# One more pair of query tiles computed ahead, and a list scheduler that counts an engine's own result delay

## The chip, the cores and the metric

The kernel runs on one core of one Trainium2 chip. Time is device time of one execution in microseconds, and a kernel is given by the median of its runs; the kernel before took 1141.6 us (three runs, 1141.54 to 1143.01). TensorE (PE) does the matrix products and loads its weights on a queue of its own (PEld); VectorE (DVE), ScalarE (ACT) and GpSimd (POOL) do the elementwise work; SyncE (SP) issues most DMAs and POOL issues the accumulating ones. Each engine works through its own instructions in the order in which the program lists them, and waits on semaphores where an operand is not there yet.

## The reference

Two layers over 1024 tokens of width 1024, all in float32:

```
x = layer_norm(a*x + gla_mixer(x))          # gated linear attention, 4 heads, chunks of 64
k, v = shared_kv(x)                         # 3 groups x 2 heads of 128, rope on k
x = layer_norm(a*x + dilated_mixer(x, k, v))

def dilated_mixer(x, k, v):
    q, gate = split(x @ w_in)               # q: 3 groups x 8 heads x 128; gate: 1024
    q = rope(q) * 128**-0.5
    for g, (window, dilation) in enumerate(((128, 1), (512, 4), (2048, 16))):
        o[g], lse[g] = windowed softmax attention of q[:, g] over k[:, g], v[:, g]
    o = sum(softmax(lse over g)[g] * o[g])
    return (o * silu(gate)) @ w_out
```

The change lies in the second layer: in how `q` is projected, and in the order of the work everywhere.

## The kernel before

**Arithmetic.** A float32 product is made of three fast ones: each operand is split in a rounded upper part and the rest (`wh`, `wl` for weights, `x1h`, `x1l` for the activations), and `wh*xh + wh*xl + wl*xh` is summed in PSUM. The rest of a weight is made in one of two ways: by a subtraction on DVE or POOL (`split_lo`), or, with `added=True`, by a negated copy on ACT onto which a DMA from POOL then adds the weight from memory (line 664).

**Stages.** The gated linear attention takes the first 355 us, its layer norm and the start of the second layer run to about 440, the projections of V and sums of activation columns (`sums()`: tiles `T1` to `T4`, and `s`) to about 515. From there to 702 stand the *pairs*: two weight tiles are multiplied with all activations together by a scheme of seven products instead of eight (`load_pair` makes the weight sums, `seven` does the products, whose PSUM tiles are called `sev`). A pair takes 7 x 12 = 84 matmuls of 128x512, where two tiles one by one (`project`, PSUM tiles `acc`) take 96. Three pairs are the keys; the others are the query tiles that `EARLY` names as (head, head, group). The roped result (`rope`, into the page `pair`) goes to DRAM (`kd`, `qd`). From 702 to 1040 runs the attention, one head after another: `q_proj(u)` reads the query tiles that lie in `qd` and projects the missing ones itself; `scores(u)` makes the products with the keys (`lv`), the maxima and sums (`sts`), and sends them through DRAM (`std`) to another layout (`nat`), where the weights of the three groups (`ew`, `cw`) are made, which go back through `cwd`; `attend(u)` scales and transposes the probabilities (`ms<-ident,P`) and multiplies with V (`po`); `g_proj` projects the gate. The output projection and the last layer norm end the program.

**Order.** The program is not written in the order in which it runs. Every operation is recorded by `Sched`, with a cost per engine, its dependences, and a rank; `order` (line 263) then fills the engines like a list scheduler: of the operations that are ready it takes the one with the earliest start, then the lowest rank. An operation on another engine's result starts `pad` later than that result's end; one on a result of its own engine starts at once. `vp` operations may go to DVE or POOL, `va` and `vap` ones to ACT too, and the scheduler picks the engine. `issue` then emits all of them through one line, so the profile shows L462 for everything, and tiles are told apart by name.

Of the kernel before, what the change touches and what calls it, by code (L numbers as in the profile page):

```python
# [34 lines left out]
       ("POOL", "ACT"): 0.07, ("POOL", "DVE"): 0.07, ("POOL", "PE"): 0.08, ("SP", "POOL"): 0.15}  # L35
WEIGHTS, EVAC, WARM = 3000, 1000, 4
AHEAD = 0.35
RUNS, GATHER = 0.3, 1.0
QUEUED, ISSUE, ADDED = 2.4, 0.9, 1.7
EARLY = [(0, 1, 2), (2, 3, 2), (1, 3, 1), (4, 5, 2), (6, 7, 2), (4, 5, 1), (6, 7, 1)]  # L40


class Buf:
# [93 lines left out]


class Op:
    __slots__ = ("engs", "calls", "reads", "writes", "prio", "deps", "nuse", "cost", "t0", "t1", "eng", "func",  # L140
                 "first", "succ", "left", "seq", "port", "least")


class Sched:
# [81 lines left out]
    def depend(self):  # L226
        hist = {}
        self.bufs = []
        for i, o in enumerate(self.ops):
            deps = set()  # L230
            for views, wr in ((o.reads, False), (o.writes, True)):
                for v in views:
                    w, r = hist.setdefault(id(v.buf), ([], []))
                    lo, hi = v.span()
                    for j, l2, h2 in (w + r if wr else w):
                        if j != i and lo < h2 and l2 < hi:
                            deps.add(j)
            for v in o.writes:
                lo, hi = v.span()
                for h in hist[id(v.buf)]:  # L240
                    h[:] = [x for x in h if not (lo <= x[1] and x[2] <= hi)]
            for v in o.writes:
                hist[id(v.buf)][0].append((i,) + v.span())
            for v in o.reads:
                hist[id(v.buf)][1].append((i,) + v.span())
            o.deps = deps
            o.first = []
            for v in o.reads + o.writes:
                b = v.buf
                if b.users is None:  # L250
                    b.users = []
                    self.bufs.append(b)
                if not b.users or b.users[-1] is not o:
                    b.users.append(o)
                    o.first.append(b)
        for o in self.ops:
            o.succ, o.left = [], len(o.deps)
        for i, o in enumerate(self.ops):
            for d in o.deps:
                self.ops[d].succ.append(o)  # L260


    def order(self):
# [6 lines left out]
        for b in self.bufs:  # L270
            if True:
                t = tags.setdefault((id(b.pool), b.tag), {"bufs": b.bufs, "queue": [], "next": 0, "live": []})
# [53 lines left out]
        while n_done < len(ops):  # L326
            best = None
            for e in self.ENG:
                cand = None
                for o in ready[e]:  # L330
                    if o.t0 is not None:
                        continue
                    r = soft = o.least
                    for d in o.deps:
                        q = ops[d]
                        t = q.t1 + (0.0 if q.eng == e else self.pad.get((q.eng, e), self.lat))
                        r = max(r, t)
                        soft = max(soft, t + (AHEAD if e == "PE" and q.eng in ("ACT", "DVE", "POOL") else 0.0))
                    if o.first:
                        t = alloc_time(o)  # L340
                        r = max(r, t)
                        soft = max(soft, t + (AHEAD if e == "PE" and t > 0 else 0.0))
                    if r >= INF:
                        continue
                    k = o.engs.index(e)
                    st = max(free[e], r, port) if o.port[k] else max(free[e], r)
                    if any(max(free[q], r) <= st and c < o.cost[o.engs.index(e)] for q, c in zip(o.engs, o.cost)):
                        continue

                    key = (max(st, soft), o.prio)  # L350
                    if cand is None or key < cand[0]:
                        cand = (key, o, st)
                if cand is not None:
                    (late, pr), o, st = cand
                    if best is None or (late, pr) < best[0]:
                        best = ((late, pr), o, e, st)
            if best is None:
                left = [o for o in ops if o.t0 is None]
                raise RuntimeError(f"no instruction can be issued; {len(left)} left, first {left[0].calls[0][0]} "
                                   f"{[v.buf.name for v in left[0].writes]}")  # L360
            _, o, e, st = best
            c = o.cost[o.engs.index(e)]
            if o.func is not None and e == "ACT":
                new = act_set(o.func, cur_set)
                if new != cur_set:

                    c += 1.3 if cur_set else 0.0
                    cur_set = new
            o.t0, o.eng = st, e
            if o.calls[0][0] == "dma_start":  # L370
                added = e == "POOL"
                dma_free = max(dma_free, st + ISSUE * added) + c * (ADDED if added else 1.0)
                o.t1 = dma_free + (QUEUED if added else 1.7)
                free[e] = st + (ISSUE if added else 0.37)
            else:
                o.t1 = st + c
                free[e] = o.t1
                if o.port[o.engs.index(e)]:
                    port = o.t1
            for b in o.first:  # L380
                if b.placed:
                    continue
                b.placed = True
                tg = tags[id(b.pool), b.tag]
                tg["next"] += 1
                if len(tg["live"]) >= tg["bufs"]:
                    old = min((x for x in tg["live"] if all(u.t0 is not None for u in x.users)),
                              key=lambda x: max(u.t1 for u in x.users))
                    tg["live"].remove(old)
                tg["live"].append(b)  # L390
            for p in {id(v.buf.pool) for v in o.reads + o.writes}:
                pool_users[p]["left"] -= 1
                pool_users[p]["end"] = max(pool_users[p]["end"], o.t1)
            for q in o.engs:
                ready[q].remove(o)
            for s in o.succ:
                s.left -= 1
                if s.left == 0:
                    for q in s.engs:
                        ready[q].append(s)  # L400
            done.append(o)
            n_done += 1
# [216 lines left out]
def trunk(tc, xT, wP, wA, wA12, wAv3, w2, wO, wK, wV0, wV12, wB, wOB, par_d,  # L619
# [10 lines left out]
    t1 = S.pool("t1", side="right")  # L630
# [15 lines left out]
    def hs(half):  # L646
        return slice(half * 512, half * 512 + 512)
# [36 lines left out]
    def project(piece, xs, evac, halves=(0, 1), added=False):  # L684
        w = load_w(piece, added)
        for half in halves:
            acc = ps.tile([128, 512], F32, name="acc", bufs=2)
            proj_cols(w, xs, hs(half), acc)
            with S.later(-EVAC):
                evac(half, acc)  # L690
# [495 lines left out]
    vd0 = [dram.tile([128, T], F32, name=f"vd0{c}") for c in range(2)]  # L1186
    qd = {(u, g): dram.tile([128, T], F32, name=f"qd{u}{g}") for *us, g in EARLY for u in us}

# [20 lines left out]
    def layer_b(xs, early):  # L1209
# [17 lines left out]
        def rope(pg, g, half, acc):  # L1227
            r = hs(half)
            t1 = small("t1", "t1", 2)
            S.vector.tensor_mul(t1, acc, cosT[:, r])  # L1230
            t2 = small("t2", "t2", 2)
            S.scalar.copy(t2[0:64, :], acc[64:128, :])
            S.scalar.copy(t2[64:128, :], acc[0:64, :])
            S.vp.tensor_mul(t2, t2, sinT[:, r])
            S.vp.tensor_add(to_group(pg, g, half), tok_view(t1, g), tok_view(t2, g))
# [166 lines left out]
        jobs = [((wK[2 * g], kd[0][g]), (wK[2 * g + 1], kd[1][g]), g) for g in range(3)]  # L1402
        jobs += [((wB[u, g], qd[u, g]), (wB[v, g], qd[v, g]), g) for u, v, g in EARLY]
        w = load_pair([a[0] for a in jobs[0][:2]], True)
# [34 lines left out]
        def q_proj(u):  # L1439
            Q = [page(p0, F32, "Q") for _ in range(3)]  # L1440
            U[u]["Q"] = Q
            for g in range(3):
                if (u, g) in qd:
                    S.sync.dma_start(Q[g], qd[u, g])
                else:
                    project(wB[u, g], xs, lambda half, acc: rope(Q[g], g, half, acc), added=True)


        def g_proj(u):
# [293 lines left out]
    for kt in range(NK):  # L1743
        wf = wts.tile([128, 1024], F32, name="wf", bufs=2)
        q = p1 if kt < 4 else p0
# [102 lines left out]
```

## Time and profile before

| what | value |
|---|---|
| median of the runs | 1141.6 us |
| the profiled execution's own time | 1139.95 us |
| its span, first to last instruction | 1137.9 us |
| TensorE busy | 1122.0 us, 99% |
| VectorE busy | 838.2 us, 74% |
| ScalarE busy | 590.0 us, 52% |
| GpSimd busy | 190.3 us, 17% |
| moved by DMA | 143.80 MB, mean 126 GB/s |

The profile is one execution. Its waits name for each engine what it waited for; its chain follows the work that ended last back to the start, with the start and length of each piece; its timeline lists the instructions of one engine in a window, with consecutive equal ones put together and the idle time before them in brackets. A matmul of 128x512 is shown with 0.39 us from start to end, but matmuls overlap: a row of the chain, length by count, gives the time from one to the next.

### The profile page before, as it was taken

The page shows a single profiled execution, that of the slowest core. Times are in us where ns is not written, and L with a number is a line of the kernel's source. Part 1 is how long each engine was busy: PE and PEld are TensorE (multiplying, and loading weights), DVE is VectorE, ACT ScalarE, POOL GpSimd, SP SyncE. Part 2 cuts the span into 40 slices and gives each one's busy share as a digit, 9 for nine tenths or more (in the row PEclk, how much of TensorE's full clock was granted, in tenths as well). Part 3 has the DMA queues.
Part 4 walks back from the last instruction along what each step waited for, and adds up shares of the span by engine and source line. Part 5 has one row for each costly group of instructions (what it writes and reads, how often), then busy time and mean ns, then how long its engine had stood idle before and what let it go on. Part 6 is the DMA issues. An engine that isn't in the chain of part 4 may idle for free.

```text
span 1137.9 us, 20061 instructions
## 1 busy us (share of the span) xinstructions
PE 1122.0 (99%) x7660; PEld 953.9 (84%) x7660; DVE 838.2 (74%) x1663; ACT 590.0 (52%) x1183; POOL 190.3 (17%) x187
## 2 busy tenths in 40 slices
PE   9999999999999999999999999999999999999997
PEld 9888888888987887887888888878888888988886
DVE  6286963686968599988898987558676778867578
ACT  5355532545564244555656565566654666633242
POOL 1000000100122021222223232021321113312000
PEclk9999999999999999999999999999999999999999
DMA  8111122211242453955556568653535553342544
GB/s 266 64 39 39 57 94 74 93 58 38 75 174 95 139 172 136 273 164 153 149 142 172 130 174 247 167 113 68 122 95 135 146 121 80 80 136 84 175 134 182
DMA packets 106191, 143.80 MB, mean 126 GB/s; under 512 B 45072, under 2 KB 63376, under 8 KB 106096
## 3 DMA queue, kind: packets, MB, share of 16 engines
q1 hardware_dynamic: 99616, 126.01, 34.9%
q0 software_dynamic: 6480, 16.52, 8.2%
q8 instruction: 60, 0.98, 0.4%
q14 instruction: 35, 0.29, 0.1%
HBM read 111.89 MB, written 30.61 MB: 125 GB/s over the span
## 4 chain that ended last, share of the span: by engine, by line
PE 84%; DVE 8%; DMA 3%; ACT 2%; issue 1%; POOL 0%; SPq 0%; DVEq 0%; ACTq 0%; POOLq 0%
PE acc L462 41%; PE sev L462 15%; PE po L462 9%; PE lv L462 8%; PE vac L462 5%; PE ms L462 3%; PE pro L462 3%; DVE rt L462 2%; DVE wl L462 1%; DMA wf<-in_wOB 1%; DVE x1l L462 1%; DVE P L462 1%; DMA wf<-in_wK 1%; ACT wh L462 1%; DMA ogf<-ogB 1%
## 5 line engine op out<-in xcount | busy, mean ns | idle before, releaser
L462 ACT ACTIVATE wh<-wf 128x1024 fp32r<-128x1024 f32 (+3 forms) x114 | 105.6, 928 | 150.6 <-PE acc L462 100.9
L462 PE MATMUL acc<-x1h,wh 128*128 128x512 f32 x288 | 126.7, 440 | 0.0
L462 PE MATMUL acc<-x1h,wl 128*128 128x512 f32 x288 | 113.0, 392 | 0.0
L462 PE MATMUL acc<-x1l,wh 128*128 128x512 f32 x288 | 112.4, 390 | 0.0
L462 DVE TENSOR_TENSOR wl<-wf,wh 128x1024 fp32r<-128x1024 f32 (+3 forms) x62 | 74.8, 1208 | 46.8 <-ACT wh L462 36.6
L462 PE MATMUL acc<-xh,wh 128*128 128x512 f32 x256 | 102.0, 398 | 0.0
L462 PE MATMUL acc<-xl,wh 128*128 128x512 f32 x256 | 99.8, 390 | 0.0
L462 PE MATMUL acc<-xh,wl 128*128 128x512 f32 x256 | 99.8, 390 | 0.0
L462 PE MATMUL sev<-T,wh 128*128 128x512 f32 x320 | 98.9, 389 | 0.5 <-DVE T L462 0.5
L462 ACT ACTIVATE P<-P,sts 128x256 f32<-128x256 f32 (+1 forms) x128 | 59.8, 468 | 30.3 <-DVE sts L462 28.5
L462 PEld LDWEIGHTS sev<-T,wh 128*128 128x128 f32 x320 | 60.0, 188 | 13.3 <-DVE T L462 0.9
L462 PE MATMUL lv<-K,Q 128*64 128x64 f32 (+2 forms) x512 | 70.6, 287 | 0.6 <-DVE sts L462 0.5
L462 POOL DMA_DIRECT2D wl<-in_wB x39 | 34.5, 909 | 192.8 <-ACT wl L462 174.5
L462 PEld LDWEIGHTS acc<-x1h,wl 128*128 128x128 f32 x288 | 54.0, 188 | 12.0
L462 PEld LDWEIGHTS lv<-K,Q 128*128 128x128 f32 (+1 forms) x512 | 53.6, 163 | 11.9 <-DVE sts L462 2.1
L462 PE MATMUL sev<-T,wl 128*128 128x512 f32 x160 | 62.3, 389 | 0.0
L462 PEld LDWEIGHTS acc<-x1l,wh 128*128 128x128 f32 x288 | 54.4, 189 | 8.7
L462 PEld LDWEIGHTS acc<-x1h,wh 128*128 128x128 f32 x288 | 54.3, 189 | 8.6
L462 DVE CUSTOM_DVE_ANT_0 P<-lv,bmask 128x256 f32<-128x256 f32 (+1 forms) x128 | 47.0, 379 | 18.2 <-PE lv L462 16.9
L462 PE MATMUL acc<-ogh,wh 128*128 128x512 f32 x152 | 60.1, 396 | 0.1
L462 PE MATMUL acc<-ogl,wh 128*128 128x512 f32 x152 | 59.3, 390 | 0.2 <-POOL ogl L462 0.2
L462 PE MATMUL acc<-ogh,wl 128*128 128x512 f32 x152 | 59.2, 390 | 0.0
(298 smaller groups left out, 2926.2 us busy)
## 6 DMA issues: line engine op xcount, KB each, us to landing
wf<-in_wB SPq DMA_DIRECT2D x32, 512.0 KB
wf<-in_wA SPq DMA_DIRECT2D x24, 512.0 KB
wl<-in_wB POOLq DMA_DIRECT2D x18, 512.0 KB, 8.0
wf<-in_wO SPq DMA_DIRECT2D x16, 512.0 KB
wf<-in_wOB SPq DMA_DIRECT2D x16, 512.0 KB
qd<-pair SPq DMA_DIRECT2D x14, 512.0 KB
Q<-qd SPq DMA_DIRECT2D x14, 512.0 KB
wf<-in_wV SPq DMA_DIRECT2D x12, 512.0 KB
```

The costliest lines, as they stand in the source:

```text
L462: getattr(handle[o.eng], meth)(*[conv(a) for a in args], **{k: conv(v) for k, v in kw.items()})
```

## The change

Three edits in one:

```
--- before.py
+++ after.py
 AHEAD = 0.35
+OWN = {"PE": 0.0, "SP": 0.0, "DVE": 0.115, "ACT": 0.11, "POOL": 0.1}
-EARLY = [(0, 1, 2), (2, 3, 2), (1, 3, 1), (4, 5, 2), (6, 7, 2), (4, 5, 1), (6, 7, 1)]
+EARLY = [(0, 1, 2), (2, 3, 2), (0, 1, 1), (2, 3, 1), (4, 5, 2), (6, 7, 2), (4, 5, 1), (6, 7, 1)]
...
-            deps = set()
+            deps, o.raw = set(), set()
...
                         if j != i and lo < h2 and l2 < hi:
                             deps.add(j)
+                            if not wr:
+                                o.raw.add(j)
...
-                        t = q.t1 + (0.0 if q.eng == e else self.pad.get((q.eng, e), self.lat))
+                        t = q.t1 + (OWN[e] * (d in o.raw) if q.eng == e else self.pad.get((q.eng, e), self.lat))
...
-                    project(wB[u, g], xs, lambda half, acc: rope(Q[g], g, half, acc), added=True)
+                    project(wB[u, g], xs, lambda half, acc: rope(Q[g], g, half, acc), added=u > 0)
```

`EARLY` has eight pairs, so that all sixteen tiles of groups 1 and 2 are made ahead, and `q_proj` projects one tile per head (8 in all, where it were 10). `OWN` makes the scheduler start an operation that reads a result of its own engine a little after that result's end. And one tile's `wl`, that of head 0 in group 0, is made by subtraction. The engines' programs differ nearly everywhere. In all, POOL gets 192 elementwise operations and DMAs before and 214 now, DVE 1665 and 1648, ACT 993 and 1009, SP 498 and 502 DMAs. Among POOL's new ones are ten `pair<-t,t` of 128x512, one for each pair but one, and a second `wl<-wf,wh` of 128x1024 close to the V projections' middle.

Three places in the order matter below. The first is the V projections and `sums()`, where transposes (`ms`) are copied from PSUM into `x1r`. DVE before:

```order
L462 TENSOR_TENSOR T30_4865<-rt_4085,T30_4865 128x512
L462 TENSOR_TENSOR T20_4873<-rt_4278,T20_4873 128x512
L462 TENSOR_TENSOR x1l5_4399<-rt_4330,x1h5_4386 128x512
L462 TENSOR_TENSOR x1l6_4426<-rt_4379,x1h6_4412 128x512
L462 COPY x1r_4897<-ms_4809 128x512
L462 TENSOR_TENSOR rt_4435<-rt_4435,R_4641 128x512
L462 TENSOR_SCALAR rt_4435<-rt_4435,par_321 128x512
```

ACT now, at the same place:

```order
L465 ACTIVATE x1h6_4399<-rt_4375 128x512
L465 ACTIVATE x1h7_4442<-rt_4433 128x512
L465 ACTIVATE T10_4874<-old_4764 128x512
L465 ACTIVATE x1r_4878<-ms_4780 128x512
L465 ACTIVATE T30_4884<-rt_4085 128x512
L465 ACTIVATE T20_4890<-rt_4266 128x512
L465 ACTIVATE wh_4921<-wf_4829 128x1024
```

Of the eight copies into `x1r` DVE did five and ACT three; now DVE does two and ACT six. The third copy, which stood behind two `x1l` subtractions on DVE, stands behind `T10` on ACT, and `T10`'s operand `old_4764` is made by DVE.

The second is ACT at the end of the second pair of keys. `u1` and `u2` are copies of the products' PSUM tiles, `wh<-wf` and `wh<-sum` belong to the weights of the pair after. ACT before:

```order
L462 ACTIVATE wh_5439<-wf_5368 128x512
L462 ACTIVATE wl_5445<-wf_5368 128x512
L462 ACTIVATE t2_5450<-u1_5306 64x512
L462 ACTIVATE wh_5439<-sum_5437 128x512
L462 ACTIVATE t2_5450<-u1_5306 64x512
L462 ACTIVATE u1_5466<-sev_5391 128x512
L462 ACTIVATE u2_5474<-sev_5417 128x512
L462 ACTIVATE s4_5481<-sum_5472 128x512
```

ACT now:

```order
L465 ACTIVATE u1_5427<-sev_5400 128x512
L465 ACTIVATE s4_5439<-sum_5432 128x512
L465 ACTIVATE wh_5447<-wf_5334 128x512
L465 ACTIVATE u2_5453<-sev_5421 128x512
L465 ACTIVATE wl_5458<-wf_5334 128x512
L465 ACTIVATE wh_5447<-sum_5405 128x512
L465 ACTIVATE t2_5473<-u1_5310 64x512 x2
```

The copy `u1` came behind the next pair's `wh<-wf` and `wh<-sum`; now it stands ahead of them.

The third is SP at the end of the last pair. Before:

```order
L462 DMA wf_6904<-in_wB 128x1024
L462 DMA qd71_6946<-pair_6929 128x1024
L462 DMA qd61_6985<-pair_6865 128x1024
L462 DMA wf_7011<-in_wB 128x1024
L462 DMA Q_7017<-qd02_6021 128x1024
L462 DMA V02_7020<-vd30_4619 64x1x512 x2
```

Now:

```order
L465 DMA wf_7077<-in_wB 128x1024
L465 DMA qd71_7122<-pair_7105 128x1024
L465 DMA qd61_7145<-pair_7033 128x1024
L465 DMA Q_7150<-qd01_6349 128x1024
L465 DMA Q_7154<-qd02_6011 128x1024
L465 DMA V02_7159<-vd30_4619 64x1x512 x2
```

Two query tiles of head 0 are read back behind the last writes, where it was one, with no weight load between. On PE 105 `acc` matmuls stood between the last product of the last pair and the first score, and now 75. Between the last score of head 0 and the transposes of its probabilities PE had 75 `acc` matmuls and, of head 1's scores, the sixteen small ones and 16 larger; now it has 45, the sixteen small ones and 7 larger. On SP two weight loads stood between the `nat<-std` reads of head 0; now these reads stand together, ahead of the next weight load, and behind two reads of query tiles for head 1.

More of the change, by code (lines that the diff above doesn't have):

```diff
@@ L139 @@
 class Op:
-    __slots__ = ("engs", "calls", "reads", "writes", "prio", "deps", "nuse", "cost", "t0", "t1", "eng", "func",
+    __slots__ = ("raw", "engs", "calls", "reads", "writes", "prio", "deps", "nuse", "cost", "t0", "t1", "eng", "func",
                  "first", "succ", "left", "seq", "port", "least")
```

## The prediction

> **What bounds the kernel now.** I read the page's busy times first, then the windows by stage, then what TensorE waited for, then the chain.
>
> ```profile
> span 1137.9 us, 20061 instructions
> PE 1122.0 (99%) x7660; PEld 953.9 (84%) x7660; DVE 838.2 (74%) x1663; ACT 590.0 (52%) x1183; POOL 190.3 (17%) x187
> ...
> core 0: us, PE busy (x) PEld busy (x) DVE busy (x) ACT busy (x) POOL busy (x), PEclk, DMA share, GB/s
> 440.00:515.00 75.00, 72.06 (x413) 62.43 (x412) 66.54 (x103) 41.35 (x73) 13.82 (x8) 0.98 0.63 193
> 515.00:702.00 187.00, 185.17 (x815) 152.97 (x816) 158.58 (x218) 113.86 (x192) 54.45 (x50) 1.00 0.61 164
> 702.00:1040.00 338.00, 335.97 (x2085) 289.58 (x2084) 240.07 (x780) 199.28 (x596) 74.00 (x96) 1.00 0.47 114
> ```
>
> TensorE has work in 99% of the span, and in both stages that the new pair touches: 185.17 of 187 us in the pairs, 335.97 of 338 in the attention. VectorE is next, with 158.58 and 240.07. So only two things can save time: fewer or shorter matmuls, and fewer of TensorE's few stalls. The stalls are single events:
>
> ```profile
> PE ms L462 <- DVE x1r L462: 2.3, 1, 2.3
> PE sev L462 <- ACT u L462: 1.5, 1, 1.5
> PE po L462 <- DVE diag L462: 0.8, 1, 0.8
> ```
>
> The columns are the total, the number of times and the longest. For the price of a matmul I use the chain, whose pieces are start, length and count:
>
> ```profile
> 540.05 162.14 PE sev L462 x714
> 702.19 23.80 PE acc L462 x105
> 725.99 1.50 PE lv L462 x34
> ```
>
> 162.14 / 714 = 0.2271 us and 23.80 / 105 = 0.2267 us from one 128x512 matmul to the next.
>
> **The matmuls.** The eighth pair adds 7 x 12 = 84 matmuls, and two tiles of 96 / 2 = 48 times two, 96 in all, leave the attention. Net 12 fewer: 12 x 0.2269 = **-2.72 us**, certain as long as TensorE sets the pace in both stages. What lies beside it: ten pairs cost VectorE 158.58 us in a stage of 187, so a pair keeps it some 15.9 us (an upper bound, since the stage's start holds other work), under the pair's own 84 x 0.2271 = 19.1 us on TensorE; the new one is covered with 3 us to spare, and without that cover each us would count once per pair. The attention loses 96 x 0.2267 = 21.8 us of TensorE's work and the rotary products of two tiles on VectorE; 336 - 22 = 314 us of TensorE stand against less than 240 of VectorE. The two more tiles that go through DRAM are four transfers of 512 KB, 2 MB beside a stage share of 0.47 to 0.61 of the DMA engines: no price as throughput, a possible one as latency (below). The subtraction for head 0's first weights replaces an ACT copy and an accumulating DMA by one VectorE operation, which takes 1.24 us in this row of the chain:
>
> ```profile
> 492.82 1.24 DVE wl L462
> ```
>
> VectorE is free for 98 of the attention's 338 us, so I cost it at nothing, and at 1.2 us if it is late.
>
> **The stall at 478.** This is what the scheduler's new delay can move most. The timeline of VectorE, GpSimd and TensorE there:
>
> ```profile
> 476.61 3.46 DVE L462 TENSOR_TENSOR x1l<-rt,x1h 128x512 fp32r<-128x512 f32 x2
> 476.94 2.59 POOL L462 TENSOR_TENSOR wl<-wf,wh 128x1024 fp32r<-128x1024 f32 x1 [5.25 <-ACT wh L462]
> 480.00 0.68 DVE L462 COPY x1r<-ms 128x512 f32<-128x512 f32 x1
> 480.83 0.84 PE L462 MATMUL ms<-ident,rt 128*128 128x128 f32 x4 [2.34 <-DVE x1r L462]
> 481.31 0.77 PE L462 MATMUL vac<-wh,x1h 128*128 128x512 f32 x1
> ...
> 482.56 0.69 DVE L462 TENSOR_TENSOR x1l<-rt,x1h 128x512 fp32r<-128x512 f32 x1 [0.43 <-ACT x1h L462]
> 484.45 0.43 PE L462 MATMUL vac<-wl,x1h 128*128 128x512 f32 x1
> ```
>
> A subtraction `x1l` takes 0.69 us alone; the two of them beside GpSimd's subtraction took 3.46, 2.1 more than twice 0.69. The copy that frees the transposes' bank stood behind them on VectorE, and TensorE stood still for 2.34 us. Then comes a second price:
>
> ```profile
> 481.00:484.50 3.50, 3.50 (x12) 2.82 (x11) 2.39 (x6) 0.63 (x1) 0.00 (x0) 0.51 0.99 339
> 484.50:488.00 3.50, 3.50 (x17) 2.91 (x16) 1.08 (x1) 2.07 (x3) 0.00 (x0) 1.00 0.46 157
> ```
>
> The granted clock (third from the end) is 0.51 for 3.5 us. From 481.31 to 484.45 seven matmuls started in 3.14 us, where 7 x 0.227 = 1.59: 1.55 us lost. Together 2.34 + 1.55 = 3.9 us. The 1.5 us stall below is followed by no such window.
>
> In the new order this copy is on ACT, and `x1l` no longer stands ahead of it; the copies that ACT has taken are away from the engine that GpSimd slows. But GpSimd's 128x1024 subtraction now stands some 25 matmuls earlier, beside VectorE's `old`, `rt` and `T10`, and ACT's copy stands behind `T10`. Bounds: nothing is left of the stall (-3.9), or VectorE loses the same 2.1 us there and everything stays (0). ACT is busy 41 of 75 us in this stage and VectorE 66.5, so the copy has moved to the engine with room; I take 0.9 us as left: **-3.0 us**.
>
> The Trainium skill, in "TensorE: Matmul & The Clock Gate", section "What's actually happening", puts the drop to half clock behind an idle window of about 3.4 us. By that, a stall of 2.34 us would cost only itself and the term would be about -1.4 instead of -3.0. The trace disagrees: clock 0.51 behind 2.34 us.
>
> **The stall at 540.** In the second pair TensorE waits for ACT's copy of the first product (`u`):
>
> ```profile
> 526.68 1.38 SPq L462 DMA_DIRECT2D wf<-in_wK  x2
> 536.34 1.72 POOL L462 TENSOR_TENSOR sum<-wf 128x512 f32<-128x512 f32 x1 [6.37 <-DMA wf<-in_wK]
> 538.09 0.63 ACT L462 ACTIVATE wh<-sum 128x512 fp32r<-128x512 f32 x1 [2.00 <-POOL sum L462]
> 539.40 1.09 ACT L462 ACTIVATE u<-sev 128x512 f32<-128x512 f32 x2
> ```
>
> The next pair's weights are issued at 526.68 and land some 9.6 us later; GpSimd sums them, ACT waits 2.00 us for the sum, and `u` stands behind. In the new order `u1` stands ahead of `wh<-wf` and `wh<-sum`. What is late next is VectorE, which now makes both sums between its rotary products; it may stand 1 to 2 us for the weights, with 3 us of room a pair. Bounds -1.5 and 0 (VectorE's turn to hold the PSUM tiles); nearest is the row of the waits, since the cause is gone from ACT's queue: **-1.3 us**.
>
> **The start of the attention.** Here the change takes cover away: 75 matmuls instead of 105 before the first score, 45 instead of 75 before head 0's probabilities are transposed.
>
> ```profile
> 706.31 5.42 SPq L462 DMA_DIRECT2D qd<-pair  x2
> 710.29 1.09 DVE L462 TENSOR_TENSOR pair<-t,t 128x512 f32<-128x512 f32 x1
> 715.34 0.38 SPq L462 DMA_DIRECT2D Q<-qd  x1
> ...
> 748.53 1.25 SPq L462 DMA_DIRECT2D std<-sts  x2
> 749.82 2.71 SPq L462 DMA_DIRECT2D nat<-std  x3
> 756.03 0.33 SPq L462 DMA_DIRECT2D wf<-in_wB  x1
> 756.42 1.51 SPq L462 DMA_DIRECT2D nat<-std  x2
> 764.31 0.19 DVE L462 TENSOR_REDUCE cw<-nat 128x8 f32<-128x24 f32 x1
> 766.39 0.69 DVE L462 TENSOR_TENSOR P<-P,ew 128x512 f32<-128x512 f32 x1
> ```
>
> The query reads stand on SP behind the last page's write, which ended 706.31 + 5.42 = 711.73, that is 9.5 us after the last product (702.19). Both reads are then issued by some 10.5, and I have no row for their landing; the two weight loads above bound it at 9.6 us together. So they land between 13 (the shortest load that the chain shows, 2.71 us for `x1t<-x1r`, whose row is 489.02) and 20 us behind the last product; the first score is due at 75 x 0.2267 = 17.0. Bounds 0 and 3 us.
>
> ```profile
> 489.02 2.71 DMA x1t<-x1r
> ```
>
> Then the group weights: from the first `std` write (748.53) to `P<-P,ew` (767.08) passed 18.6 us, of which a weight load held the queue from 752.53 to 756.03, and VectorE came to the reduction late. Without that the trip is some 4 us to the last read's issue, 2.7 or more to landing and 2.8 from the reduction to the product's end, plus one for the second write: 11 us or so. Between the last score and the transposes TensorE now has 45 x 0.2267 = 10.2 us, 1.5 us for the small scores and some 2 for seven larger ones, 13.7, of which 2 pass before the write. The margin is about nothing: bounds 0 and 5 us. For both places I take **+1.2 us**, nearer to the lower ends, since TensorE stood only 0.8 us at `po<-diag` before.
>
> **Everything else** is reordered too. The stalls not named so far, but for the program's start and end, were short ones of under 1 us, spread over the span, and a new order draws them anew; I put **+0.3 us** and +-1.5.
>
> **Sum**: -2.72 - 3.0 - 1.3 + 1.2 + 0.3 = -5.5 us against the profiled execution: 1139.95 - 5.5 = 1134.4. The median of the runs lay 1141.6 - 1139.95 = 1.65 above that execution, and I expect the same offset: **1136.1 us**. The case's own range is 1133.5 to 1139.
>
> **The rivals.**
>
> *Only the matmuls count.* The stall of the V projections is not removed but moves: GpSimd's subtraction (2.59 us) slows VectorE's `old`, `T10` waits, ACT's `x1r` copy waits behind it, and TensorE stands for 2 us or more and loses 1.55 at half clock; the pair's stall goes over to VectorE's sums. 1141.6 - 2.7 = 1138.9, between 1138 and 1141. For it: the 3.46 us row, and ten more GpSimd operations on pages in the pairs. Against: the copy's new engine is less than 60% busy.
>
> The Trainium skill says in "GPSIMD Engine Reference", section "Specifications", that GpSimd's SBUF interfaces are shared with VectorE and that VectorE instructions with two SBUF inputs contend; it speaks against moving work to GpSimd, as this rival does. The trace agrees: 3.46 us for two subtractions that take 0.69 each alone.
>
> *Slower: the round trips through DRAM are no longer covered.* The first score waits 3 us for the query tile, the clock drops as at 481 (1.55), and head 0's weights come 5 us late with another 1.55: 11.1 us. With the gains elsewhere, 1141.6 - 2.7 - 3.0 - 1.3 + 11.1 = 1145.7. It decides from 9.3 us on (7.0 eaten plus 2.3). For it: 30 fewer matmuls, 6.8 us of cover, gone at each of two places. Against: `nat` is no longer cut by weight loads, and the query reads no longer stand behind one.
>
> *Better: nothing new stalls.* Both stalls go entirely and the start costs nothing: -2.7 - 3.9 - 1.5 - 0.5 = -8.6, 1133.0.
>
> **How the numbers follow.** Forecast 0.54, only the matmuls 0.25, slower 0.14, better 0.07. Changes under 0.2% (2.3 us, 1139.3 to 1143.9) can hardly be told from none. Faster: all of forecast and better, but 0.02, and 0.13 of the second case: 0.72. Slower: 0.10 of the third case, since its price may be half; the rest, 0.18, is no change. The range takes in the second case and half of the way to the third: 1132.0 to 1142.0.
>
> **What would show it.** In the new profile: TensorE 12 matmuls fewer and its busy time some 4 us lower (2.7, and the half clock); in the windows between 470 and 490 a granted clock of 1.00; among the waits no `ms <- x1r` over 1 us and no `sev <- u`; the attention's stage some 22 us shorter and the pairs' 19 longer. Wrong would be: a window with a clock near 0.5 after 500, or waits `lv <- Q` and `ms <- P` or `po <- diag` of 2 us and more at the first head, which is the slower case; or a wait of `sev` for VectorE's `sum`, `c` or `u` in the pairs.

## The result: 1128.4 us, 1.2% faster

The changed kernel takes 1128.44 us (1127.46 to 1128.91, four runs) beside 1142.3 (1141.54 to 1143.54) for the kernel before: ratio 0.9876, 95% interval 0.9859 to 0.9894. A second measurement (below, "the changed kernel again") gives 1128.14 and 0.9898 (0.9882 to 0.9914). The sign was forecast with 0.72; 1128.4 lies below the range of 1132 to 1142. One run of the kernel before, 1878.36 us at a granted clock of 0.556, is left out of the ratios and ranges below.

The page's head, of the kernel after:

```profile
span 1127.1 us, 20068 instructions
PE 1115.3 (99%) x7648; PEld 950.0 (84%) x7648; DVE 826.0 (73%) x1646; ACT 597.7 (53%) x1199; POOL 214.4 (19%) x209
```

The profiled execution took 1128.91 us, 11.0 less than the profiled one of before (1139.95); spans differ by 10.8. All that TensorE waited for over 0.15 us at a time (total, times, longest):

```profile
PE lv L465 <- DVE sts L465: 1.8, 5, 0.6
PE pro L465 <- DVE Dg L465: 1.3, 1, 1.3
PE acc L465 <- POOL wol L465: 1.0, 1, 1.0
PE ms L465 <- DVE sum L465: 0.2, 1, 0.2
PE ms L465 <- DVE sq L465: 0.2, 1, 0.2
```

The waits for `x1r` and for `u` are gone. Windows of the same stages in both kernels show where the time came from. Before, the V projections with `sums()`, then the pairs:

```profile
432.50:506.00 73.50, 70.71 (x397) 61.13 (x397) 65.67 (x101) 38.46 (x65) 12.21 (x8) 0.98 0.65 202
506.00:702.00 196.00, 194.03 (x866) 160.29 (x865) 166.55 (x231) 119.13 (x203) 56.07 (x51) 1.00 0.60 161
```

After, the same two, between the same events:

```profile
431.30:503.10 71.80, 71.58 (x421) 63.01 (x420) 66.13 (x94) 45.02 (x77) 18.91 (x11) 1.00 0.66 206
503.10:712.60 209.50, 209.50 (x926) 173.46 (x925) 170.15 (x247) 126.71 (x218) 58.52 (x57) 1.00 0.61 162
```

Together they took 269.5 us and now 281.3, with 84 matmuls or 19.1 us more in them: 7.3 us gained. TensorE stood still for 4.8 us in them before, and stands still for 0.2 us now (length less the first number behind it, its busy time). The chain of the kernel after shows all eleven pairs as one piece without a gap:

```profile
503.30 209.47 PE sev L465 x924
712.76 17.00 PE acc L465 x75
729.76 1.50 PE lv L465 x34
```

209.47 / 924 = 0.2267 us a matmul. The rest of the account, from where the same events stand in both traces: the program's start 0.6 us shorter (by the clock's record it is at full speed 4.4 us behind the start, where it was 6.6; in a second profile of the changed kernel it is at 7.3, so this part is chance), the first layer 0.6 shorter, the attention 22.2 shorter, of which 96 matmuls are 21.8, the last stage 0.8 longer (`acc` waits 1.0 for GpSimd's `wol`, which the second profile doesn't show). 0.6 + 0.6 + 7.3 - 19.1 + 22.2 - 0.8 is the 10.8 of the spans.

### The profile page after: what moved, and what is told of

Read it like the earlier page. It is cut to its first block, busy times and chain, and to the rows that moved or that the text cites. A ratio compares the mean times of both kernels' runs of the same rounds, so it can differ in the third digit from the quotient of the medians.

```text
span 1127.1 us, 20068 instructions
## 1 busy us (share of the span) xinstructions
PE 1115.3 (99%) x7648; PEld 950.0 (84%) x7648; DVE 826.0 (73%) x1646; ACT 597.7 (53%) x1199; POOL 214.4 (19%) x209
## 4 chain that ended last, share of the span: by engine, by line
PE 91%; DVE 4%; DMA 2%; ACT 2%; issue 1%; POOL 0%; SPq 0%; DVEq 0%; ACTq 0%
PE acc L465 42%; PE sev L465 19%; PE po L465 9%; PE lv L465 8%; PE vac L465 7%; PE ms L465 4%; PE pro L465 2%; DMA wf<-in_wOB 1%; DVE P L465 1%; DVE rt L465 1%; DVE wl L465 1%; DVE t L465 0%; DMA xf<-in_xT 0%; DVE x1l L465 0%; ACT t L465 0%
## 5 line engine op out<-in xcount | busy, mean ns | idle before, releaser
L465 PE MATMUL acc<-x1h,wh 128*128 128x512 f32 x256 | 114.0, 445 | 0.0
L465 PE MATMUL sev<-T,wh 128*128 128x512 f32 x352 | 108.3, 389 | 0.0
L465 PE MATMUL acc<-x1h,wl 128*128 128x512 f32 x256 | 100.6, 393 | 0.0
L465 PE MATMUL acc<-x1l,wh 128*128 128x512 f32 x256 | 100.1, 391 | 0.0
L465 PEld LDWEIGHTS sev<-T,wh 128*128 128x128 f32 x352 | 66.1, 188 | 13.7
L465 PE MATMUL sev<-T,wl 128*128 128x512 f32 x176 | 68.5, 389 | 0.0
L465 POOL TENSOR_TENSOR wl<-wf,wh 128x1024 fp32r<-128x1024 f32 x10 | 24.2, 2418 | 181.4 <-PE ms L465 91.5
L465 PEld LDWEIGHTS acc<-x1h,wl 128*128 128x128 f32 x256 | 48.0, 188 | 10.8
L465 PEld LDWEIGHTS acc<-xh,wl 128*128 128x128 f32 x256 | 48.1, 188 | 10.3
```

The costliest lines, as they stand in the source:

```text
L465: getattr(handle[o.eng], meth)(*[conv(a) for a in args], **{k: conv(v) for k, v in kw.items()})
```

## The experiments

Each kernel was timed beside the kernel before on its own chip, and ratios go by that. The kernel before spread widely in all of them: 1136.5 to 1145.3 us in one group, 1138.5 to 1143.9 and 1137.2 to 1143.5 in the others, where the changed kernel's eight runs lie within 1127.5 to 1128.9.

### The order alone, the pair alone

The first leaves out the pair and the flag:

```
-EARLY = [(0, 1, 2), (2, 3, 2), (0, 1, 1), (2, 3, 1), (4, 5, 2), ...]
+EARLY = [(0, 1, 2), (2, 3, 2), (1, 3, 1), (4, 5, 2), ...]
-    project(..., added=u > 0)
+    project(..., added=True)
```

> Leaves the pairs at seven and head 0's weights as they were, and has only the scheduler's result delay (OWN). Theory A: nearly all beyond the 12 matmuls comes from the order, the stalls at 478, 515 and 540 us and what hangs on them: 1142.3 - (13.9 - 2.7) = about 1131, between 1130 and 1133, with no wait of ms for x1r and no wait of sev for u. Theory B: the delay by itself only moves stalls about, and they went because the eighth pair shifted the program: 1138 to 1142.

Measured: 1133.37 (1130.39 to 1134.93), ratio 0.9937 (0.9917 to 0.9958), -7.0 us. The second has the new `EARLY` in the kernel before, nothing else.

> Has the eighth pair and nothing else: old scheduler, old way for head 0's weights. Theory A: the order up to the pairs is that of before, so the waits ms for x1r (2.3 us) and sev for u (1.5 us) stay, and only 12 matmuls go: -2.7 us, 1139 to 1140. Theory B: the pair moves the order enough to lose the stalls: 1132 to 1136.

Measured: 1137.64 (1134.15 to 1142.18), ratio 0.9977 (0.9961 to 0.9992), -2.75 us. Its waits are those of before:

```profile
PE ms L462 <- DVE x1r L462: 2.3, 1, 2.3
PE sev L462 <- ACT u L462: 2.0, 1, 2.0
```

The interval for the pair alone is wide, 0.9 to 4.4 us of gain: it agrees with the 12 matmuls, and that its median meets their 2.72 is luck in part, since its profile has waits that before lacks (`acc` 1.1 us for `sg`, `u` 0.5 us longer). By the waits the two stalls stay with the pair alone and go with the scheduler's delay alone: theory A in both. The order alone came out 0.4 us above theory A's range of 1130 to 1133, and its profile has one stall that neither before nor after shows, at 886 us in the attention:

```profile
PE ms L465 <- DVE PT L465: 2.3, 2, 2.1
```

### One instruction moved: the stall at 478

On VectorE, in the kernel before, the copy `x1r` goes ahead of the two subtractions it stood behind; all else is as it was:

```
+        ahead("x1r", 2, "DVE", "x1l5")     # the third x1r copy of VectorE, to before x1l5
         done.sort(key=lambda o: (o.t0, o.seq))
```

> The kernel before with one instruction moved: on VectorE the copy x1r that TensorE waited for stands ahead of the two x1l subtractions instead of behind them; every other engine's order is unchanged. Theory A: the 2.34 us stall and the half clock behind it (1.55 us) go, -3.9 us, with a granted clock of 1.00 from 481 to 484.5. If this is also the place where runs of the kernel before differ from one another (1141.5 to 1143.5, the profiled one 1139.95), the median falls by 4 to 6 and the spread shrinks. Rival: GpSimd's subtraction slows whatever stands beside it and the stall only changes its name: 0 to -1.5 us.

Measured: 1137.87 (1135.13 to 1139.98), ratio 0.9979 (0.9966 to 0.9992), -2.5 us; the profiled execution took 1138.1. VectorE's timeline, then two windows (the granted clock is the third number from the end):

```profile
476.13 0.68 DVE L470 COPY x1r<-ms 128x512 f32<-128x512 f32 x1
476.73 3.32 DVE L470 TENSOR_TENSOR x1l<-rt,x1h 128x512 fp32r<-128x512 f32 x2
```

```profile
481.00:484.50 3.50, 3.50 (x17) 2.88 (x17) 3.07 (x7) 2.70 (x4) 0.00 (x0) 1.00 0.96 342
997.50:1001.00 3.50, 3.28 (x15) 3.09 (x16) 2.92 (x7) 0.00 (x0) 1.41 (x2) 0.59 0.21 75
```

The copy no longer waits, TensorE no longer stalls, and the clock stays up, though the subtractions take as long as before (3.32 against 3.46). In this execution another wait came, at 997 us (`po <- PT`, 2.3 us), with the half clock behind it. The trace decides for theory A at this place. The time alone would not: its interval, 0.9 to 3.9 us of gain, just reaches theory A's 3.9, and leaves out no gain at all but not the rival's 1.5. The spread shrank little (standard deviation 1.4 us in twelve runs, 1.9 in 29 of before). The next experiment moves, beside this copy, ACT's `u1` ahead of the next pair's `wh<-sum`.

> As the run with the copy moved, and on ACT the copy u1 of the second pair ahead of the next pair's wh<-sum. Theory A: another 1.5 to 1.7 us less than with the one copy moved, -5.5 us against before, no wait of sev for u. Rival: the weights that land late are then waited for by VectorE, whose sums and rotary products hold the PSUM tiles: the second move gives 0 to 0.5 us.

Measured: 1138.08 (1134.29 to 1140.61), ratio 0.9974 (0.9961 to 0.9987), -2.3 us: no different from the one move. In both profiles the wait of `sev` for `u` was 0.3 us or less, so in the profile the second move had nothing left to take: the rival's number, but not its reason. Whether the first move took this stall along is not shown: without either move it is 0.7 us in two other profiles below, so its length varies by itself. What the copy `u1` alone is worth stays open. Both have the wait at 997.

### The same stall, by taking GpSimd away

In the kernel before, GpSimd's 128x1024 subtraction at 477 becomes VectorE's, directly behind the copy:

```
+        g.eng, g.t0 = "DVE", c.t0 + 1e-4     # g: GpSimd's wl subtraction; c: the x1r copy
```

> The kernel before with one instruction moved from GpSimd to VectorE: the 128x1024 subtraction that ran beside the x1l subtractions at 477, now on VectorE directly behind the x1r copy; every other order is unchanged. Theory A (GpSimd's instruction holds VectorE until it ends, and that made the stall): x1l takes 0.69 us again, the copy starts at about 478 and TensorE waits 0.7 us or less for it, without half clock, -3.2 us in a profile and -1.5 to -3.5 in the median. Rival (VectorE is simply late there, with or without GpSimd): the stall stays over 1.5 us, and the time within 1 us of before.

Measured: 1138.31 (1135.36 to 1141.44), ratio 0.998 (0.9967 to 0.9993), -2.25 us. VectorE's and TensorE's timeline:

```profile
475.70 1.29 DVE L467 TENSOR_TENSOR x1l<-rt,x1h 128x512 fp32r<-128x512 f32 x2
476.90 0.69 DVE L467 COPY x1r<-ms 128x512 f32<-128x512 f32 x1
477.50 1.22 DVE L467 TENSOR_TENSOR wl<-wf,wh 128x1024 fp32r<-128x1024 f32 x1
...
477.74 0.63 PE L467 MATMUL ms<-ident,rt 128*128 128x128 f32 x4
```

Without GpSimd beside them the two subtractions take 1.29 us instead of 3.46, the copy starts 3.1 us sooner, and TensorE does not wait. Theory A: GpSimd's instruction held VectorE, and what stood behind on VectorE made it a stall.

### The kernel before, a second profile

> The kernel before unchanged, for a second profile of it. Theory A: the stalls at 478 and 540 are there again with the half clock behind the first, and what differs between its runs is whether a further wait of about 2.3 us, as the one at 997 us in the two kernels with moved copies, comes with its own half-clock window. Theory B: the two stalls are of that one profiled run, and are missing or elsewhere here.

It took 1142.16 us. Three of its waits, a piece of its chain, and two windows:

```profile
PE po L462 <- DVE PT L462: 3.0, 1, 3.0
PE ms L462 <- DVE x1r L462: 2.3, 1, 2.3
PE sev L462 <- ACT u L462: 0.7, 1, 0.7
```

```profile
989.32 8.15 DMA ogf<-ogB
```

```profile
481.00:484.50 3.50, 3.50 (x18) 2.95 (x18) 2.41 (x6) 0.87 (x2) 0.00 (x0) 1.00 1.01 337
1001.50:1005.00 3.50, 3.50 (x15) 3.31 (x16) 2.72 (x5) 0.00 (x0) 1.42 (x2) 0.51 0.24 75
```

Both theories had a part. The stall at 478 is there again, 2.3 us, but this time with no half clock behind it; the one at 540 had shrunk to 0.7. And there is a wait of 3.0 us at 1001, with half clock, where the first profile shows 0.15. Its cause is a read of `ogB` for the output projection, 8.15 us in the chain (6.12 in the first profile's chain): ACT's `ogh` waits for it, VectorE's `ogl` for ACT, and `PT` stands behind `ogl`. So that read's landing differs between the two executions. The granted clock, which is recorded for every run, says how much of the spread goes with half clock: over the 56 runs of before in the three groups, the nine with a mean clock of 0.995 took 1143.1 us on average and the ten with 0.999 took 1139.7, where one window of 3.41 us at half clock takes 0.0015 off the mean. At which places these windows came in the runs without a profile is not known. The changed kernel's eight runs have 0.998 or 0.999, and its profiles have no wait at this place.

### The changed kernel again, and without the flag

> The changed kernel once more, on the chip and beside the runs of the kernel before that the runs of this group share. The parts alone measured -7.2 us (order only, 0.9937) and -2.7 us (pair only, 0.9977) against a kernel before whose runs spread from 1136.5 to 1145.3. Theory A: the parts add, the ratio is 0.990 to 0.992 and the first 0.9876 was helped by slow runs of before. Theory B: the parts need each other, the ratio is again 0.987 to 0.989.

Measured: 1128.14 (1127.96 to 1128.5), ratio 0.9898 (0.9882 to 0.9914): between the theories, -11.4 us on this chip. The next one changes `added=u > 0` back to `added=True` in the changed kernel.

> The changed kernel with head 0's lower weights made as before (negated copy and an accumulating DMA). Theory A: the flag is worth nothing by itself, within 1 us of the changed kernel. Theory B: it is what the two parts alone lack, and this run is 2 to 4 us slower than the changed kernel.

Measured: 1131.81 (1130.34 to 1134.26), ratio 0.9932 (0.9915 to 0.9948), 3.7 us slower than the changed kernel. Theory B by the number. The kernel without the flag has the order and the pair, and is no better than the order alone (0.9937), so the pair's 2.7 us don't show there; the intervals allow either. The profile names a stall as the cost, far from the flag's own DMA. VectorE, GpSimd and TensorE at 881 us, and a window behind:

```profile
881.12 4.02 DVE L465 COPY_PREDICATED P<-above,P 128x128 f32<-128x128 uint8 x2
882.01 2.76 POOL L465 TENSOR_TENSOR Q<-t,t 128x512 f32<-128x512 f32 x2
885.62 1.06 PE L465 MATMUL ms<-ident,P 128*128 128x128 f32 x4 [2.12 <-DVE PT L465]
```

```profile
885.70:889.00 3.30, 3.30 (x12) 2.94 (x13) 2.35 (x10) 1.80 (x7) 0.00 (x0) 0.50 0.96 323
```

This is the stall that the order alone had too, there without half clock. In the changed kernel the order is another at this place: of the two rotary sums only one is GpSimd's, VectorE is held for less long, and TensorE has no such wait:

```profile
880.53 3.20 DVE L465 COPY_PREDICATED P<-above,P 128x128 f32<-128x128 uint8 x2
881.39 1.55 POOL L465 TENSOR_TENSOR Q<-t,t 128x512 f32<-128x512 f32 x1
```

To test that, the two sums go to VectorE in the kernel without the flag:

```
+        for i in (6, 7):            # GpSimd's sums into Q at 882 us
+            q[i].eng = "DVE"
```

> The kernel without the flag (head 0's weights as before, 1131.8 us) with two rotary sums Q<-t,t at 882 us moved from GpSimd to VectorE, nothing else. Theory A: they held VectorE's copy_predicated for 3.5 us, TensorE's wait for PT (2.1 us) and the half clock behind it are all that the flag's absence costs; both go, and the time is that of the changed kernel, 1128 to 1129. Rival: the flag itself, the accumulating DMA at the attention's start, costs the time: 1131 to 1132 stays.

Measured: 1129.42 (1127.63 to 1131.39), ratio 0.9899 (0.9883 to 0.9916), 2.4 us less by the medians and 3.8 by the ratios; the wait at 886 and its half clock are gone:

```profile
885.70:889.00 3.30, 3.30 (x29) 3.18 (x28) 2.87 (x11) 2.33 (x11) 0.00 (x0) 1.00 1.02 336
```

Theory A, nearly to the full amount, though the median stays 1.3 us above the changed kernel's 1128.14: most of the flag's gain is where GpSimd's work falls, not the weights it is about.

### Less cover

> The changed kernel with a ninth pair, the group 0 tiles of heads 6 and 7 (all other edits kept): 12 matmuls fewer again. Theory A (TensorE's count sets the time): -2.7 us against the changed kernel, 1125 to 1126. Rival (the projections were cover for the softmax round trips of heads 6 and 7, which have few other matmuls beside them): 0 to +5 us, with waits of lv, ms or po in the last two heads.

Measured (`(6, 7, 0)` added to `EARLY`): 1134.24 (1132.99 to 1136.45), ratio 0.9952 (0.9936 to 0.9968), 6.1 us slower than the changed kernel, a little more than the rival's upper end. At head 7, with half clock behind:

```profile
PE ms L465 <- ACT P L465: 2.2, 1, 2.2
PE po L465 <- DVE diag L465: 1.9, 1, 1.9
```

With two shorter new waits these are 5.6 us; with 1.7 lost in a window of 3.4 us at half clock, and 2.7 gained by the 12 matmuls, that makes 4.6, and its profiled execution is 4.5 us slower than the second one of the changed kernel (1133.02 beside 1128.5). The rival's mechanism is shown: ahead of the transposes at head 7 VectorE scales the probabilities, and waits for the group weights to come back from DRAM.

```profile
1031.95 2.45 DVE L465 TENSOR_SCALAR P<-P,cw 128x128 f32<-128x128 f32 x10 [1.59 <-DMA cw<-cwd]
```

> The changed kernel with the group 0 tiles of heads 0 and 1 as the ninth pair instead: no projection matmul is left between head 0's scores and the transposes of its probabilities (45 in the changed kernel, 75 before). If the prediction's slower case is a real mechanism that only had room to spare, TensorE now waits 5 to 15 us there, at a granted clock near 0.5 behind it, and the time is 5 to 18 us above the changed kernel. If the round trips through DRAM are hidden anyway, it is 2.7 us below.

Measured (`(0, 1, 0)` instead): 1146.96 (1146.57 to 1149.18), ratio 1.0062 (1.0042 to 1.0081), 18.8 us above the changed kernel. TensorE's timeline, then the windows:

```profile
758.82 2.70 PE L465 MATMUL lv<-K,Q 128*64 128x64 f32 x34 [3.54 <-DMA Q<-qd]
777.87 2.70 PE L465 MATMUL lv<-K,Q 128*64 128x64 f32 x34 [4.50 <-DMA Q<-qd]
```

```profile
758.50:768.00 9.50, 8.42 (x50) 6.36 (x50) 4.33 (x33) 6.10 (x30) 0.19 (x1) 0.50 0.77 217
775.50:785.00 9.50, 6.37 (x45) 5.07 (x46) 3.22 (x28) 4.77 (x25) 0.00 (x0) 0.50 0.26 45
```

The first score waits 3.54 us for the query tile, head 1's 4.50, and with each TensorE has half its clock for 10.24 us, three times the 3.41 of a single window. Small matmuls with waits between them follow there; that these keep the clock down is likely, but not shown. So the first half of the prediction's slower case, a score that waits for its query tile, is real. The second half, transposes that wait for the group weights, shows at head 7 with nine pairs (above), but not at head 0: here the transposes began without a wait, 0.2 us behind the product with head 0's group weights,

```profile
789.17 0.63 PE L465 MATMUL ms<-ident,P 128*128 128x128 f32 x4
```

and what TensorE waited for between them and head 0's scores was mostly head 1's query tile.

### A faster version

In the changed kernel three rotary sums, at 739, 758 and 881 us, go from GpSimd to VectorE, by the same edit with other indices.

> The changed kernel with three rotary sums Q<-t,t (at 739, 758 and 881 us) moved from GpSimd to VectorE, each of which held a VectorE instruction for 1.2 us and more just ahead of a wait lv for sts (0.6, 0.6, 0.8 us). Theory A (holding is the cause of those waits): -1 to -2 us against the changed kernel's 1128.1. Rival (VectorE's own load makes them): 0 to +0.7 us, since VectorE gets 0.7 us more work three times.

Measured: 1126.52 (1125.14 to 1126.99), ratio 0.987 (0.9853 to 0.9887). That is 1.6 us below the changed kernel by the medians, and no run of the one is within the runs of the other, though they ran in different groups; by the ratios it is 0.7 or 3.2 us, after the changed kernel's first or second measurement, and the first difference is within the intervals. The first row is GpSimd's and the second VectorE's in the changed kernel, the third VectorE's in this one, the same instruction:

```profile
739.51 1.64 POOL L465 TENSOR_TENSOR Q<-t,t 128x512 f32<-128x512 f32 x1
739.79 1.92 DVE L465 TENSOR_TENSOR t<-t,sinT 128x512 f32<-128x512 f32 x1 [0.47 <-ACT t L465]
```

```profile
741.43 0.69 DVE L469 TENSOR_TENSOR t<-t,sinT 128x512 f32<-128x512 f32 x1 [0.47 <-ACT t L469]
```

The waits of `lv` for `sts` fell from 1.8 us to 0.2, which is the size of the gain:

```profile
PE lv L469 <- DVE sts L469: 0.2, 1, 0.2
```

Theory A by the trace, and the time agrees with it.

## Why the prediction was right in sign and wrong in size

1136.1 us was forecast and 1128.44 came, 7.7 less. About 3.0 of that lie in the V projections and the pairs, 1.6 in the attention, 0.9 in the rest, and 2.1 in the offset between profile and median. The mechanism held, and the steps that failed are sizes: what was kept as left of the stalls, what was added for new ones, and the offset.

**The matmuls: right.** The pair alone gave -2.75 us (0.9 to 4.4), where -2.72 was worked out, and the new pair lies wholly under TensorE (209.50 of 209.50 us busy). The room beside VectorE was read from 515 on, though the pairs begin at 506.0: 166.55 us for ten pairs are 16.7 a pair, and 2.4 us to spare, not 3. It was enough.

**The stall at 478: right cause, too small.** The term was -3.0, since 0.9 us were kept for GpSimd's earlier subtraction. That collision did come. GpSimd, VectorE, ACT and TensorE after:

```profile
469.58 2.40 POOL L465 TENSOR_TENSOR wl<-wf,wh 128x1024 fp32r<-128x1024 f32 x1 [3.86 <-DMA x1t<-x1r]
469.96 2.58 DVE L465 TENSOR_TENSOR old<-rt,old 128x512 f32<-128x512 f32 x1
472.57 0.63 ACT L465 ACTIVATE T<-old 128x512 fp32r<-128x512 f32 x1 [1.77 <-DVE old L465]
473.10 0.58 ACT L465 ACTIVATE x1r<-ms 128x512 f32<-128x512 f32 x1
474.59 0.60 PE L465 MATMUL ms<-ident,rt 128*128 128x128 f32 x4
```

VectorE's `old` took 2.58 us instead of 0.69, ACT waited 1.77 us with `T`, and the `x1r` copy stood behind, word for word the rival's chain; but the copy was done at 473.68, 0.9 us before the transposes that need the bank. The step that failed is the 0.9 us of stall kept for this: it measured 0, and the whole 3.9 went.

**The stall at 540, and the one at 515.** -1.3 was forecast for the first; it went entirely (1.5 us in the first profile of before, 0.7 in the second). The 0.5 us for `T` in the first pair was put under "everything else" and went too. The two stages gave 7.3 us where 4.3 were counted; 3.9 + 1.5 + 0.5 are 5.9 of these, and the other 1.4 stand in no single wait. The step "what is late next is VectorE" cost nothing: the pairs' 209 us have no gap. So, in hindsight, the likeliest case should have been the one called better, all stalls gone, for the waits named each of them as a single event with a cause in another engine's queue; at 1133.0 it would still have been 4.6 us too slow. That the new order drew no new stall over 1 us in the pairs and the attention is luck in part: the order alone, and the order and pair without the flag, each drew one of 2.1 us at 886.

**The start of the attention: wrong by its sign.** +1.2 us was taken, with bounds 0 and 8. The attention in all came out 0.4 us better than its 96 matmuls. The reads of the query tiles on SP, the end of the group weights on VectorE and the transposes on TensorE, after:

```profile
720.06 1.18 SPq L465 DMA_DIRECT2D Q<-qd  x2
763.14 0.68 DVE L465 TENSOR_TENSOR P<-P,ew 128x512 f32<-128x512 f32 x1
763.88 0.66 PE L465 MATMUL ms<-ident,P 128*128 128x128 f32 x4
```

The first score came at 729.76, 17.0 us behind the last product (75 matmuls), without a wait, so the query tile had landed within 9.7 us of its read's issue. The group weights were finished at 763.82 and the transposes began at 763.88: the margin was as thin as the prediction said, and it held. That the mechanism exists is shown by the run with no cover, 18.8 us slower, for the query tile, and by the one with nine pairs, at head 7, for the group weights. The step that failed is the +1.2 us: both waits measured 0. It took a point inside the bounds for waits that come only when the cover falls short.

**Everything else: +0.3 forecast.** Outside the two stages and the attention -0.4 was measured: the start and the first layer 0.6 each, against 0.8 in the last stage. The clock reached full speed between 4.4 and 7.3 us behind the start in four profiles of the two kernels, so part of this is chance. The 0.5 for `T` and the untraced 1.4 us above were to come under this term too.

**The offset between profile and median: wrong.** 1.65 us were added to the new profile's time because the runs of before lay above theirs. The second profile of before shows one reason: a wait of 3.0 us at 1001, with half clock behind it, that the first one hardly had. In the changed kernel this wait is absent, and the median of its runs lies 0.5 us under the profiled one. Of the 13.9 us of the first comparison 11.0 are in the profiles and 2.8 in these offsets; in the second comparison the difference is 11.4. How much of the offset is that one wait, and how much chance, stays open.

By the sums: -5.5 was forecast in the profile and -11.0 came. By the medians the pair alone gave 2.75 us, the order alone 7.0, both without the flag 7.7, and all three 11.4. The parts do not add, since each changes which stalls come; the flag, costed at nothing, was worth 3.7 us, most of it through the order.

## What to carry to other kernels

On a program in which one engine is busy 99% of the time, read its few waits one by one, and price each with what may follow it, here a half-speed clock for 3.4 us or more behind nine of the twelve stalls over 2 us. When a change reorders work, a stall can go as a whole, as the one at 478 did, or come as a whole, as the one at 886, so keep two cases rather than a mean. Before an elementwise operation is put on GpSimd "because it is idle", look at which two-input VectorE operations run beside it and what stands behind those; three such sums moved back to VectorE made this kernel faster, although VectorE got more to do.

## What the runs showed of the hardware that was not expected

**GpSimd's two-input instruction doesn't slow VectorE, it holds it.** In the two profiles of before and after, 101 VectorE operations with two SBUF inputs (`TENSOR_TENSOR`) began while a GpSimd `TENSOR_TENSOR` was running. 83 of them, of 128x512, ended 0.54 to 0.65 us behind GpSimd's end, whatever the time at which they began, a little less than the 0.69 us that one takes alone; 11 others, of 128x1024, ended about 1.1 behind it (alone they take 1.22). Six smaller ones ended 0.3 or less behind it, and one alone ended before it. None of the 44 with an input in PSUM was lengthened, and none of 43 PSUM copies. `copy_predicated` on SBUF can be held over two GpSimd instructions in a row: two of 0.3 us took 4.02 in the run without the flag.

**When the clock drops is not a matter of the stall's length alone.** Nine stalls of TensorE lasted 2.1 to 2.4 us. Half clock followed in the first profile of before (2.34), the pair alone (2.33), both kernels with moved copies (2.27 and 2.37), the kernel without the flag (2.12) and the one with nine pairs (2.23), and not in the second profile of before (2.32), in the order alone (2.13), and at 903 us in the run without cover (2.14): six of nine. Behind stalls of 2.0 us or less it did not come, and with the three of 3.0 to 4.5 us it did. The Trainium skill, in "TensorE: Matmul & The Clock Gate", section "What's actually happening", has the activity counted in windows of about 3.4 us that run freely. Behind these stalls the half clock did last 3.41 us, or in the run without cover three times that, and its coming behind one stall of 2.3 us and not behind another agrees with windows that don't start with the stall. That an idle window of 3.4 us is needed does not agree: 2.12 us was enough.
